# Two rounds per token gather, halved ranking matrices, nineteen weight slots and twelve rounds in an expert layer

## The chip, the cores and the metric

The kernel runs on one core of one Trainium2 chip. The metric is the time of one execution in device microseconds; the time of a kernel is the median of several executions.

## What is computed

A streaming encoder of two layers over one sequence of 256 tokens of width 1024, in fp32. The first half of each layer (band attention, a state space model, retention, one projection in and one out) is called the mixing stage here and is not changed. The second half is a hierarchical mixture of 32 experts:

```python
def _hier_moe(h, w_group, b_group, w_expert, b_expert, w_gate, w_up, w_down):
    ...
    expert_id = group_idx[:, None] * EXPERTS_PER_GROUP + top_idx        # two experts of one group per token
    combine = jnp.sum(jax.nn.one_hot(expert_id, N_EXPERTS, dtype=f32) * top_w[..., None], axis=1)
    ...
        hg = jnp.einsum('nd,edf->nef', t, w_gate[e])
        hu = jnp.einsum('nd,edf->nef', t, w_up[e])
        act = jax.nn.silu(hg) * hu * combine[:, e, None].astype(t.dtype)
        out = out + jnp.einsum('nef,efd->nd', act, w_down[e]).astype(f32)
```

An expert's weights are 3 MiB (gate and up 1024 x 256 each, down 256 x 1024), so a layer's experts are 96 MiB, and every one is read once.

## The kernel before

Weights reach the core as tiles of 128 x 2048 fp32, 1 MiB each: two for an expert's gate and up (`load_gu`, line 131, its two halves of the contraction) and one for its down projection (`load_wd`, line 138). SP issues these loads one after another, in an order that the framework sets. A tile goes into one of 17 slots in turn (`wslot`, line 121): 8 of the pool tag `ring2`, 7 of a ring that the mixing stage uses as well, 2 of the tag `ring3`. The slots of the two tags lie on memory that the mixing stage used just before; a slot is free again when the matmuls that read it are done. In layer 0 the first eight slots first hold tiles for the next layer's modulation.

A round handles 128 token slots: two experts of up to 64 tokens each, or four light ones of up to 32. `route` picks each token's two experts and each token's place in its expert's list (`posm`), all on VectorE with a few matmuls; TensorE and VectorE work there in the order written. `order` counts tokens per expert on the device and ranks the experts that are not in fixed order, with comparison matrices of 26 x 26 per partition (lines 1081 to 1092): the six largest are heavy, the other 20 light. Six experts (`FIX`) are taken in fixed order, so their weights can be loaded before the ranking is known. `ORDER` gives eleven rounds: three fixed, then light and heavy in turn three times, then two light.

Rounds are grouped in blocks whose tokens are gathered together. `matrix` builds a 0/1 selection matrix on VectorE, `gathered` multiplies it with the token rows, which are kept as two fp32r parts (`xhi`, `xlo`), eight chunks of 128 model columns, four matmuls each; ScalarE and VectorE carry the result out of PSUM with norm and modulation applied. Block 0 is the three fixed rounds (256 columns before round 0, 128 more after its gate/up), blocks 1 and 2 are four rounds each, 512 columns.

Per round, TensorE then does `slots` (two transposes that give each slot's weight `cw` and the mask `sT`), `gate_up` (fp32, experts side by side in columns of the array), `turned` (two transposes of the activations, behind ScalarE's silu and VectorE's product), `down`, and `scatter`. Before a scatter, `outputs` multiplies with the gate row on VectorE, rounds to fp32r on ScalarE and subtracts on VectorE; `scatter` multiplies both parts with the mask, and VectorE adds the result to `x`. The order on TensorE in `run` is written by hand; the other engines are ordered by the framework there. Behind a round's gate/up come the scatter and the down of earlier rounds. Between the first and the second half of the rounds stands `overflow`: all engines load the largest count and skip, or take, a branch for experts with more tokens than slots.

PSUM has four tags of two banks: gate/up and activations turn in one, down in another, and gathers, scatters and transposes share the tags `tr` and `ac`.

Of the kernel before, what the change touches and what calls it, by code (L numbers as in the profile page):

```python
# [12 lines left out]
F32R = mybir.dt.float32r  # L13
# [12 lines left out]

FIX, HEAVY, LIGHT = 6, 6, 32
DYN = NE - FIX
ORDER = ["fixed"] * 3 + ["light", "heavy"] * 3 + ["light"] * 2
EPS = 1e-6  # L30
PRIO = 200
NW = 7
NW2 = 8
NW3 = 2

# [16 lines left out]
def body(tc, I, O):  # L52
# [3 lines left out]
    with tc.tile_pool(name="cp", bufs=1) as cp, tc.tile_pool(name="ring", bufs=NW) as ring, \  # L56
# [3 lines left out]
        def nm(s):  # L60
# [6 lines left out]
                        "mx": 4, "smx": 4},  # L67
                "moe": {"ring2": NW2, "ring3": NW3, "big": 2, "b4": 1, "b2": 8, "y2": 4, "b1": 8, "cw": 3},
                "prep": {"b1": 4}}
# [887 lines left out]
        def route(l, filler, scaled):  # L957
# [5 lines left out]
            def turned(h, t):  # L963
                xT[h, t] = b2([128, 512])
                p = ps("tr")
                for c in range(4):
                    PE.transpose(p[:, c * 128:(c + 1) * 128], x[:, t, (4 * h + c) * 128:(4 * h + c + 1) * 128], ident)
                return p
# [50 lines left out]
            m1, at1, f1 = first_max(ev, "a")  # L1019
            oh1, oh2 = sb([128, 10, 8], "oh1"), sb([128, 10, 8], "oh2")  # L1020
            V.tensor_tensor(oh1, at1, wide(f1), op=ALU.is_equal)
# [24 lines left out]

            def weights():
                V.tensor_tensor(oh2, at2, wide(f2), op=ALU.is_equal)
                m5 = m1.rearrange("p (t g) -> p t g", t=2)
# [13 lines left out]
                V.tensor_tensor(w2, w1, e, op=ALU.mult)  # L1063
                wa, both = sb([128, 10, 8], "wa"), sb([128, 10, 8], "both")
                for o, oh, w in ((wa, oh1, w1), (both, oh2, w2)):
# [5 lines left out]
            def order():  # L1071
# [8 lines left out]
                V.scalar_tensor_tensor(key, cnt[:, FIX:NE], 64.0, own, op0=ALU.mult, op1=ALU.subtract)  # L1080
                sq = [128, DYN, DYN]
                tmp, oh = sb(sq, "sqa"), sb(sq, "sqb")

                rank = sb([128, DYN], "rank")
                V.tensor_tensor(tmp, key[:, None, :].to_broadcast(sq), key.unsqueeze(2).to_broadcast(sq), op=ALU.is_ge)
                V.tensor_reduce(rank, tmp, axis=AX.X, op=ALU.add)
                V.tensor_tensor(oh, C("iota")[:, 0:DYN].unsqueeze(2).to_broadcast(sq),
                                rank[:, None, :].to_broadcast(sq), op=ALU.is_equal)

                def sorted_(dst, src):  # L1090
                    V.tensor_tensor(tmp, oh, src[:, None, :].to_broadcast(sq), op=ALU.mult)
                    V.tensor_reduce(dst, tmp, axis=AX.X, op=ALU.add)

# [29 lines left out]
        def experts(posm, comb, xhi, xlo, a2, sh2, gr2, l, ahead=True, D0=None, between=None, order=None, more=True,  # L1123
# [8 lines left out]
            if ahead:  # L1132
                numi, posd, comd = order
                _, num = nc.values_load_multi_w_load_instructions(
                    numi[0:1, :], engines=(mybir.EngineType.SP,), min_val=FIX, max_val=NE - 1,
                    skip_runtime_bounds_check_because="sums of a permutation's 0/1 rows times FIX..NE-1")
                at_ = {"fixed": 0, "heavy": FIX, "light": FIX + HEAVY}
                for r, kind in enumerate(ORDER):
                    i, n, w = at_[kind], *((4, LIGHT) if kind == "light" else (2, CAP))
                    at_[kind] += n  # L1140
                    blk, po = (0, r) if i < FIX else (1 + (r - FIX // 2) // 4, (r - FIX // 2) % 4)
                    j = slice(i - FIX, i - FIX + n) if i >= FIX else slice(i, i + n)
                    pos, cmb = (posd[:, :, j], comd[:, :, j]) if i >= FIX else (posm[:, :, j], comb[:, :, j])
                    rounds.append((blk, po * 128, w, pos, cmb, [num[e - FIX] if i >= FIX else e for e in range(i, i + n)]))
            else:
                for r in range(16):
                    j = slice(2 * r, 2 * r + 2)
                    rounds.append((r // 4, r % 4 * 128, CAP, posm[:, :, j], comb[:, :, j], [2 * r, 2 * r + 1]))
            last = {r[0]: i for i, r in enumerate(rounds)}

            def gather(blk):
                Dm[blk] = b4([128, 2, 512], F32R)
                for b, po, w, pos, _, _ in rounds:
                    if b == blk:
                        matrix(Dm[blk], po, pos, w)
                gathered(blk, slice(0, rounds[last[blk]][1] + 128), 1)

            def gathered(blk, ss, n):
                pc = {}
                w = ss.stop - ss.start  # L1160
                for c0 in range(0, 8, n):
# [8 lines left out]
                    for c in range(c0, c0 + n):  # L1170
                        if (blk, c) not in hg:
                            hg[blk, c] = b2([128, 512])
                        h = hg[blk, c][:, ss]
# [5 lines left out]
            def slots(r):  # L1179
# [11 lines left out]
                V.tensor_reduce(cw, tp[:, 0:256], axis=AX.X, op=ALU.add)  # L1191
                sT = b1_([128, 256], F32R)
                V.tensor_scalar(sT, tp[:, 0:256], 0.0, None, op0=ALU.is_gt)
# [68 lines left out]
            if not ahead:  # L1262
                for r in range(16):
                    if r % 4 == 0:
                        gather(r // 4)
                    cw, sT = slots(r)
                    scatter(sT, outputs(down(r, turned(gate_up(r, cw)))))
# [11 lines left out]
            def run(rs):  # L1279
                with tc.manual_schedule(engines={mybir.EngineType.PE}):  # L1280
                    for r in rs:
                        blk, po, _, _, _, es = rounds[r]
                        if r == 0:
                            Dm[0] = D0
                            gathered(0, slice(0, 256), 4)
                        elif po == 0:
                            for q in list(aT):
                                downs(q)
                            scatters(1)
                            gather(blk)  # L1290
                        cw, sTs[r] = slots(r)
                        act = gate_up(r, cw)
                        if r == 0:
                            gathered(0, slice(256, rounds[last[0]][1] + 128), 1)
                        scatters(0)
                        for q in list(aT):
                            downs(q)
                        aT[r] = turned(act)
                        if late and r == len(rounds) - 2:
                            late()  # L1300
                        if len(es) == 4:
                            downs(r, r == len(rounds) - 1)
                            scatters(1)
                    for q in list(aT):
                        downs(q)
                    scatters(0)

            half = last[1] + 1
            run(range(half))
# [3 lines left out]
        def moe(l, more):  # L1313
# [25 lines left out]
            with tc.manual_schedule(engines={mybir.EngineType.PE, mybir.EngineType.DVE}):  # L1339
                posm, comb, cmi, r, weights, order, less = route(l, filler, scaled)  # L1340
                D0 = b4([128, 2, 512], F32R)
                matrix(D0, 0, posm[:, :, 0:4], CAP)
                for h in range(2):
                    hs = slice(h * 512, (h + 1) * 512)
                    for t in range(2):
                        V.scalar_tensor_tensor(xlo[:, t, hs], x[:, t, hs], r[:, t:t + 1], xhi[:, t, hs].bitcast(F32),
                                               op0=ALU.mult, op1=ALU.subtract)
                matrix(D0, 4 * CAP, posm[:, :, 4:FIX], CAP)
            weights()
            ordered = order()  # L1350

            def overflow():

                n = nc.values_load(cmi[0:1, 0:1], min_val=0, max_val=S)
                with tc.If(n > CAP):
                    posr = sb([128, 2, 32], "posr")
                    V.tensor_tensor(posr, posm, less.unsqueeze(1).to_broadcast([128, 2, 32]), op=ALU.add)
# [173 lines left out]
```

## Time and profile before

| what | value |
|---|---|
| median of 3 runs | 855.92 us (855.15 to 857.68) |
| profiled execution | 861.28 us |
| its span, first to last instruction | 859.4 us |
| TensorE matmul busy | 718.6 us (84%) |
| VectorE busy | 482.2 us (56%) |
| ScalarE busy | 240.3 us (28%) |
| bytes moved | 293.62 MB, mean 342 GB/s |
| mean granted clock of TensorE | 0.927 |

The busy shares are means over the whole span. The mixing stages and the expert stages have different limits, so the rows further down are taken from stretches of the span. Times in rows are microseconds from the span's start. A matmul's row is longer than the distance to the next one, since matmuls are pipelined; durations of steps are therefore read from the start of one to the start of the next. Gate/up and down matmuls are in fp32 and each shows as two records.

### The profile page before, as it was taken

The page shows a single profiled execution, that of the slowest core. Times are in us where ns is not written, and L with a number is a line of the kernel's source. Part 1 is how long each engine was busy: PE and PEld are TensorE (multiplying, and loading weights), DVE is VectorE, ACT ScalarE, POOL GpSimd, SP SyncE. Part 2 cuts the span into 40 slices and gives each one's busy share as a digit, 9 for nine tenths or more (in the row PEclk, how much of TensorE's full clock was granted, in tenths as well). Part 3 has the DMA queues.
Part 4 walks back from the last instruction along what each step waited for, and adds up shares of the span by engine and source line. Part 5 has one row for each costly group of instructions (what it writes and reads, how often), then busy time and mean ns, then how long its engine had stood idle before and what let it go on. Part 6 is the DMA issues. An engine that isn't in the chain of part 4 may idle for free. (4 is left out here: it accounts for less than half of the span.)

```text
span 859.4 us, 11389 instructions
## 1 busy us (share of the span) xinstructions
PE 718.6 (84%) x4110; PEld 390.8 (45%) x4110; DVE 482.2 (56%) x1075; ACT 240.3 (28%) x512; POOL 115.2 (13%) x163
## 2 busy tenths in 40 slices
PE   2699999989999985987678989989699998497875
PEld 0365776675434322422126558657653532242211
DVE  6689798455654334222158989855755533422124
ACT  1534236732222110101034333494321211020102
POOL 0454150002000000000035216000100000000000
PEclk9699999997999998899898989989799999899888
DMA  9978778887998998999998846759369899899992
GB/s 370 422 302 300 260 281 352 359 290 307 374 413 345 415 416 333 415 419 414 414 417 364 315 153 251 291 211 407 140 245 418 326 417 416 342 415 420 414 416 87
DMA packets 52037, 293.62 MB, mean 342 GB/s; under 512 B 4736, under 2 KB 4992, under 8 KB 26624
## 3 DMA queue, kind: packets, MB, share of 16 engines
q1 hardware_dynamic: 49536, 287.78, 84.0%
q10 hardware_dynamic: 2432, 4.98, 1.6%
q8 instruction: 36, 0.59, 0.3%
q14 instruction: 33, 0.27, 0.1%
HBM read 289.60 MB, written 1.05 MB: 338 GB/s over the span
## 5 line engine op out<-in xcount | busy, mean ns | idle before, releaser
L1204 PE MATMUL mm<-ring,b 128*32 128x512 f32 (+1 forms) x608 | 126.8, 622 | 11.8 <-DMA ring<-in_wgu_dram 11.8
L710 DVE TENSOR_TENSOR wh<-w,wh 128x512 fp32r<-128x512 f32 x120 | 85.6, 735 | 34.7 <-ACT wh L709 34.4
L1210 DVE SCALAR_TENSOR_TENSOR b<-mm,cw,b 128x256 f32<-128x256 f32 x22 | 10.6, 483 | 160.9 <-ACT b L1208 160.9
L709 ACT ACTIVATE wh<-w 128x512 fp32r<-128x512 f32 x120 | 74.4, 629 | 87.3 <-PE mm L734 49.5
L1204 PE MATMUL mm<-w,b 128*32 128x512 f32 (+1 forms) x416 | 88.8, 631 | 8.6 <-DMA w<-in_wgu_dram 8.6
L734 PE MATMUL mm<-wh,early 128*128 128x512 f32 x288 | 78.7, 417 | 1.0 <-DVE wh L710 1.0
L1229 PE MATMUL sc<-ring,b 128*32 128x512 f32 (+1 forms) x288 | 63.4, 623 | 12.8 <-DMA ring<-in_moe_w_down_dram 8.4
L1204 PEld LDWEIGHTS mm<-ring,b 128*32 128x32 f32 (+1 forms) x608 | 34.4, 124 | 77.0 <-issue 54.8
L734 PEld LDWEIGHTS mm<-wh,early 128*128 128x128 f32 x288 | 53.1, 194 | 25.2 <-issue 6.8
L205 PE MATMUL ac<-w,cc 128*32 128x512 f32 x320 | 46.2, 662 | 20.0 <-DVE cc L199 11.6
L1208 ACT ACTIVATE b<-mm 128x256 f32<-128x256 f32 x22 | 8.4, 384 | 184.3 <-PE mm L1204 184.3
L1238 DVE TENSOR_TENSOR y<-sc,gr 128x512 f32<-128x512 f32 x44 | 30.4, 690 | 50.1 <-PE sc L1229 48.6
L1243 ACT ACTIVATE y<-y 128x512 fp32r<-128x512 f32 x40 | 25.2, 630 | 107.9 <-DVE y L1238 67.1
L729 PE MATMUL mm<-early,wh 128*128 128x256 f32 x384 | 52.5, 292 | 1.7 <-DVE wh L710 1.7
L729 PEld LDWEIGHTS mm<-early,wh 128*128 128x128 f32 x384 | 48.5, 194 | 8.3 <-issue 4.1
L1168 PE MATMUL tr<-b,big 128*128 128x512 f32 (+2 forms) x128 | 32.4, 393 | 22.8 <-DVE b L1119 20.0
L734 PE MATMUL mm<-wh,big 128*128 128x512 f32 x192 | 50.2, 414 | 1.4 <-DVE y L921 1.4
L1184 POOL TENSOR_TENSOR b<-b,comd 128x128 f32<-128x128 f32 x32 | 12.8, 424 | 282.0 <-PE mm L1216 129.9
L1204 PEld LDWEIGHTS mm<-w,b 128*32 128x32 f32 (+1 forms) x416 | 23.8, 124 | 55.4 <-issue 38.9
L1229 PE MATMUL sc<-w,b 128*32 128x512 f32 (+1 forms) x224 | 44.0, 597 | 4.8 <-DMA w<-in_moe_w_down_dram 2.9
L734 PEld LDWEIGHTS mm<-wh,big 128*128 128x128 f32 x192 | 36.7, 197 | 9.6 <-DVE y L921 2.2
L1229 PEld LDWEIGHTS sc<-ring,b 128*32 128x32 f32 (+1 forms) x288 | 15.9, 123 | 48.6 <-issue 26.8
(349 smaller groups left out, 1108.9 us busy)
## 6 DMA issues: line engine op xcount, KB each, us to landing
ring<-in_wgu_dram SPq DMA_DIRECT2D x76, 1024.0 KB, 14.6
w<-in_wgu_dram SPq DMA_DIRECT2D x52, 1024.0 KB, 13.0
w<-in_w_ada_dram SPq DMA_DIRECT2D x40, 1024.0 KB, 9.0
ring<-in_moe_w_down_dram SPq DMA_DIRECT2D x36, 1024.0 KB, 18.8
w<-in_moe_w_down_dram SPq DMA_DIRECT2D x28, 1024.0 KB, 19.5
w<-in_win_dram SPq DMA_DIRECT2D x22, 1024.0 KB, 6.9
w<-in_w_out_dram SPq DMA_DIRECT2D x8, 1024.0 KB, 7.1
ring<-in_w_ada_dram SPq DMA_DIRECT2D x8, 1024.0 KB, 11.9
```

What stands on the lines that cost most here:

```text
L205: PE.matmul(acc[32 * t:32 * t + 32, :], c1[:, k:k + 1].to_broadcast([128, 32]), w[:, t * 512:(t + 1) * 512], start=(k == 0), stop=(k == 7) ...
L709: A.activation(wh[:, 0], w, AF.Copy)
L710: lo_eng[par_[0] % len(lo_eng)].tensor_tensor(wh[:, 1], w, wh[:, 0].bitcast(F32), op=ALU.subtract)
L729: PE.matmul(pt[t][:, f * 256:(f + 1) * 256], whs[i][:, w_, fs], a[x_][:, k], start=first and f + m == 0, stop=end and m == 2, skip_group_c ...
L734: PE.matmul(pt[t], a[x_][:, k, ts_], whs[i][:, w_], start=first and m == 0, stop=end and m == 2)
L1168: PE.matmul(pc[c], (xlo if i else xhi)[:, t, cs], Dm[blk][:, t, ss], start=(i + t == 0), stop=(i + t == 3))
L1184: G.tensor_tensor(Dc[:, t].rearrange("p (e s) -> p e s", s=w), Dm[blk][:, t, po:po + 128].bitcast(F32).rearrange("p (e s) -> p e s", s=w), ...
L1204: PE.matmul(gu[o:o + w, :], hg[blk, k][:, po + o:po + o + w], ws[k // 4][j][:, k % 4] if ahead else part_gu(l, es[j], k), start=(k == 0), ...
L1210: V.scalar_tensor_tensor(act, gu[:, 256:512], cw, si, op0=ALU.mult, op1=ALU.mult)
L1229: PE.matmul(yp[h][o:o + w, :], aT[:, f * 128 + o:f * 128 + o + w], wd[j][:, f, h] if ahead else part_wd(l, es[j], f, h), start=(f == 0), s ...
L1238: V.tensor_tensor(y, yp[h], gr2[:, h * 512:(h + 1) * 512], op=ALU.mult)
L1243: A.activation(yh, y, AF.Copy)
```

## The change

Slots become 19: `ring3` has four tiles for two. Eight experts are in fixed order, in four rounds; eight heavy and sixteen light ones follow in turn, so there are twelve rounds. Every block has two rounds: six gathers of 256 columns, matrices and gathered tokens in tiles of half the size (tags `D` and `hg`). The branch stands behind block 3, round 7. The ranking uses 24 x 24 comparisons done in two halves of 12 x 24, kept in the buffers of the outputs (`y2`), where the transposed tokens of the routing now lie too. Some routing tiles reuse others' memory, masks get a tag `sT` of their own, and the tag `b1` has four buffers for eight. In `run`, a block's first round now does the pending scatter before the pending down and the gather; a light round does the pending scatter before its own down. In the last layer, `late` (the final norm's gain spread over the partitions) moves in front of the last round's gate/up.

```diff
-FIX, HEAVY, LIGHT = 6, 6, 32
+FIX, HEAVY, LIGHT = 8, 8, 32
 DYN = NE - FIX
-ORDER = ["fixed"] * 3 + ["light", "heavy"] * 3 + ["light"] * 2
+
+HALF = 3
+ORDER = ["fixed"] * 4 + ["heavy", "light"] * 4
...
-NW3 = 2
+NW3 = 4
...
-                "moe": {"ring2": NW2, "ring3": NW3, "big": 2, "b4": 1, "b2": 8, "y2": 4, "b1": 8, "cw": 3},
+                "moe": {"ring2": NW2, "ring3": NW3, "big": 2, "D": 2, "hg": 8, "y2": 4, "b1": 4, "sT": 3, "cw": 3},
...
-                xT[h, t] = b2([128, 512])
+                xT[h, t] = y2([128, 512])
...
-                sq = [128, DYN, DYN]
-                tmp, oh = sb(sq, "sqa"), sb(sq, "sqb")
+
+                H = DYN // 2
+                sq = [128, H, DYN]
+
+                def square():
+                    return y2([128, 512])[:, 0:H * DYN].rearrange("p (a b) -> p a b", a=H)
+
+                halves = [slice(0, H), slice(H, DYN)]
+                tmp, ohs = square(), [square() for _ in halves]
...
+                for hv in halves:
+                    V.tensor_tensor(tmp, key[:, None, :].to_broadcast(sq), key[:, hv].unsqueeze(2).to_broadcast(sq),
+                                    op=ALU.is_ge)
+                    V.tensor_reduce(rank[:, hv], tmp, axis=AX.X, op=ALU.add)
...
                 def sorted_(dst, src):
-                    V.tensor_tensor(tmp, oh, src[:, None, :].to_broadcast(sq), op=ALU.mult)
-                    V.tensor_reduce(dst, tmp, axis=AX.X, op=ALU.add)
+                    for hv, oh in zip(halves, ohs):
+                        V.tensor_tensor(tmp, oh, src[:, None, :].to_broadcast(sq), op=ALU.mult)
+                        V.tensor_reduce(dst[:, hv], tmp, axis=AX.X, op=ALU.add)
...
-                    blk, po = (0, r) if i < FIX else (1 + (r - FIX // 2) // 4, (r - FIX // 2) % 4)
+                    blk, po = r // 2, r % 2
...
-                Dm[blk] = b4([128, 2, 512], F32R)
+                Dm[blk] = sb([128, 2, 256], "D", F32R)
...
-                            hg[blk, c] = b2([128, 512])
+                            hg[blk, c] = sb([128, 256], "hg")
...
-                sT = b1_([128, 256], F32R)
+                sT = sb([128, 256], "sT", F32R)
...
                         elif po == 0:
+                            scatters(0)
                             for q in list(aT):
                                 downs(q)
-                            scatters(1)
                             gather(blk)
+                        if late and r == len(rounds) - 1:
+                            late()
                         cw, sTs[r] = slots(r)
                         act = gate_up(r, cw)
-                        if r == 0:
-                            gathered(0, slice(256, rounds[last[0]][1] + 128), 1)
                         scatters(0)
                         for q in list(aT):
                             downs(q)
                         aT[r] = turned(act)
-                        if late and r == len(rounds) - 2:
-                            late()
                         if len(es) == 4:
+                            scatters(0)
                             downs(r, r == len(rounds) - 1)
-                            scatters(1)
...
-            half = last[1] + 1
+            half = last[HALF] + 1
...
-                D0 = b4([128, 2, 512], F32R)
+                D0 = sb([128, 2, 256], "D", F32R)
...
-                matrix(D0, 4 * CAP, posm[:, :, 4:FIX], CAP)
```

## Rows read from the trace of the kernel before

**Rows 1.** The page, the span in 40 equal slices: what the transfers moved.

```profile
GB/s 370 422 302 300 260 281 352 359 290 307 374 413 345 415 416 333 415 419 414 414 417 364 315 153 251 291 211 407 140 245 418 326 417 416 342 415 420 414 416 87
```

**Rows 2.** Stretches, layer 1: length; PE, PEld, DVE, ACT, POOL busy; clock; DMA; GB/s.

```profile
610.00:620.00 10.00, 3.33 (x19) 2.79 (x19) 9.11 (x39) 1.53 (x4) 1.19 (x2) 0.58 0.22 92
...
629.00:700.00 71.00, 68.36 (x372) 31.05 (x368) 35.79 (x66) 13.71 (x26) 3.57 (x10) 1.00 0.93 373
700.00:845.00 145.00, 112.47 (x615) 42.02 (x616) 44.81 (x81) 16.24 (x30) 3.61 (x10) 0.92 0.96 390
```

**Rows 3.** SP's waits, whole span: us in total, times, longest us.

```profile
SPq L135 <- PE mm L1204: 56.8, 14, 13.9
SPq L143 <- PE mm L1204: 50.9, 11, 22.8
...
SPq L1355 <- SPq L1355: 39.3, 10, 12.1
```

**Rows 4.** TensorE in time: first gate/up, last scatter, layers 0 and 1.

```profile
215.85 7.09 PE L1204 MATMUL mm<-w,b 128*64 128x512 f32 x32
...
437.42 1.98 PE L1256 MATMUL ac<-y,b 128*128 128x512 f32 x4
...
625.58 7.09 PE L1204 MATMUL mm<-ring,b 128*64 128x512 f32 x32
...
845.91 1.98 PE L1256 MATMUL ac<-y,b 128*128 128x512 f32 x4
```

**Rows 5.** TensorE in time, layer 1, rounds 1 and 2.

```profile
643.69 3.60 PE L1229 MATMUL sc<-w,b 128*64 128x512 f32 x16
...
647.23 0.44 PE L1216 MATMUL mm<-cst,b 128*128 128x128 f32 x2
...
647.81 7.09 PE L1204 MATMUL mm<-w,b 128*64 128x512 f32 x32
...
654.83 0.50 PE L1258 MATMUL ac<-y,b 128*128 128x512 f32 x1
...
656.90 0.64 PE L1229 MATMUL sc<-w,b 128*64 128x512 f32 x1
```

**Rows 6.** TensorE in time, two records of the scatter ahead of the branch.

```profile
737.40 0.50 PE L1258 MATMUL ac<-y,b 128*128 128x512 f32 x1
...
740.58 0.50 PE L1259 MATMUL tr<-y,b 128*128 128x512 f32 x1 [0.58 <-DVE y L1245]
```

**Rows 7.** TensorE in time, end of a gate/up and its turn.

```profile
767.10 0.60 PE L1204 MATMUL mm<-w,b 128*32 128x512 f32 x3
...
768.86 0.44 PE L1216 MATMUL mm<-cst,b 128*128 128x128 f32 x2 [1.15 <-DVE b L1210]
```

**Rows 8.** TensorE in time: gathers of 256 columns (layer 0) and 512 (layer 1).

```profile
214.07 0.63 PE L1168 MATMUL tr<-b,big 128*128 128x256 f32 x4
214.54 0.63 PE L1168 MATMUL ac<-b,big 128*128 128x256 f32 x4
...
668.35 2.40 PE L1168 MATMUL tr<-b,big 128*128 128x512 f32 x8 [1.17 <-DVE x L1260]
...
676.08 0.38 PE L1189 MATMUL tr<-cst,b 128*128 128x128 f32 x2
```

**Rows 9.** In time, behind the branch of layer 1.

```profile
748.58 2.52 DVE L1119 TENSOR_TENSOR b<-cst,posd 128x128 fp32r<-128x128 f32 x8 [6.18 <-DVEq L1355]
...
751.05 3.75 PE L1168 MATMUL tr<-b,big 128*128 128x512 f32 x8 [9.51 <-DVE b L1119]
```

**Rows 10.** In time, routing and ranking in layer 1.

```profile
606.26 0.69 DVE L986 CUSTOM_DVE_ANT_0 y<-x 128x512 f32<-128x512 f32 x1
606.50 0.98 PE L972 MATMUL sc<-prb,b 128*128 128x40 f32 x8
...
619.59 0.85 DVE L1085 TENSOR_TENSOR sqa<-key 128x676 f32<-128x676 f32 x1
```

**Rows 11.** TensorE in time, `late` in layer 1.

```profile
807.32 1.95 PE L270 MATMUL tr<-cst 128*128 128x128 f32 x16
```

More of the change, by code (lines that the diff above doesn't have):

```diff
@@ L1019, in route @@
             m1, at1, f1 = first_max(ev, "a")
-            oh1, oh2 = sb([128, 10, 8], "oh1"), sb([128, 10, 8], "oh2")
+            oh1 = sb([128, 10, 8], "oh1")
             V.tensor_tensor(oh1, at1, wide(f1), op=ALU.is_equal)
@@ L1047, in weights @@
             def weights():
+                oh2 = sb([128, 10, 8], "aa")
                 V.tensor_tensor(oh2, at2, wide(f2), op=ALU.is_equal)
@@ L1063, in weights @@
                 V.tensor_tensor(w2, w1, e, op=ALU.mult)
-                wa, both = sb([128, 10, 8], "wa"), sb([128, 10, 8], "both")
+                wa, both = sb([128, 10, 8], "ev2"), sb([128, 10, 8], "at3")
                 for o, oh, w in ((wa, oh1, w1), (both, oh2, w2)):
@@ L1080, in order @@
                 V.scalar_tensor_tensor(key, cnt[:, FIX:NE], 64.0, own, op0=ALU.mult, op1=ALU.subtract)
-                sq = [128, DYN, DYN]
-                tmp, oh = sb(sq, "sqa"), sb(sq, "sqb")
-                rank = sb([128, DYN], "rank")
[L1085 to L1088, printed above, removed]
+                H = DYN // 2
[4 more added lines that the diff above has]
+                tmp, ohs = square(), [square() for _ in halves]
+                rank = sb([128, DYN], "rank")
+                for hv in halves:
[3 more added lines that the diff above has]
+                for hv, oh in zip(halves, ohs):
+                    V.tensor_tensor(oh, C("iota")[:, hv].unsqueeze(2).to_broadcast(sq),
+                                    rank[:, None, :].to_broadcast(sq), op=ALU.is_equal)
                 def sorted_(dst, src):
-                    V.tensor_tensor(tmp, oh, src[:, None, :].to_broadcast(sq), op=ALU.mult)
-                    V.tensor_reduce(dst, tmp, axis=AX.X, op=ALU.add)
+                    for hv, oh in zip(halves, ohs):
+                        V.tensor_tensor(tmp, oh, src[:, None, :].to_broadcast(sq), op=ALU.mult)
+                        V.tensor_reduce(dst[:, hv], tmp, axis=AX.X, op=ALU.add)
                 num = sb([128, DYN], "num")
@@ L1147, in experts @@
                     j = slice(2 * r, 2 * r + 2)
-                    rounds.append((r // 4, r % 4 * 128, CAP, posm[:, :, j], comb[:, :, j], [2 * r, 2 * r + 1]))
+                    rounds.append((r // 2, r % 2 * 128, CAP, posm[:, :, j], comb[:, :, j], [2 * r, 2 * r + 1]))
             last = {r[0]: i for i, r in enumerate(rounds)}
             def gather(blk):
-                Dm[blk] = b4([128, 2, 512], F32R)
+                Dm[blk] = sb([128, 2, 256], "D", F32R)
                 for b, po, w, pos, _, _ in rounds:
@@ L1263, in experts @@
                 for r in range(16):
-                    if r % 4 == 0:
-                        gather(r // 4)
+                    if r % 2 == 0:
+                        gather(r // 2)
                     cw, sT = slots(r)
@@ L1355, in overflow @@
                 with tc.If(n > CAP):
-                    posr = sb([128, 2, 32], "posr")
+                    posr = sb([128, 10, 8], "oh1").rearrange("p n e -> p (n e)")[:, 0:64].rearrange("p (t e) -> p t e", t=2)
                     V.tensor_tensor(posr, posm, less.unsqueeze(1).to_broadcast([128, 2, 32]), op=ALU.add)
```

## Prediction

> **What bounds the kernel now.** I read the page's slices first, then stretches of the second expert layer, SP's waits, and last the instructions in order of time. The slices show transfers near 415 GB/s through most of both expert stages, the best slice 425 or less [rows 1]. One expert tile is 1 MiB, so at 419 GB/s a load takes 1.0486/0.419 = 2.5 us, and the 96 loads of a layer 240 us. The change loads no fewer bytes; what can be won is time in which the load queue stands still.
>
> It stands still in three places. Between 610 and 620 us the queue moves 92 GB/s, because all 17 slots are full and SP waits 22.8 us for the first round's matmuls [rows 2, 3]. From 629 to 700 us TensorE is busy 68.4 of 71 us and the loads run at 373 GB/s: there TensorE is the bound, slots come free at its pace, and (419-373)/419 x 71 = 7.8 us of loading is lost; SP's wait of 13.9 us belongs to the four-round gather, during which no slot comes free [rows 2, 3]. From 700 to 845 us TensorE is busy only 112 of 145 us and the loads run at 390 GB/s, which loses 10 us, mostly at the overflow branch, where SP first lets its outstanding transfers land [rows 2, 3]. So each expert stage has a TensorE-bound head and a load-bound tail with some 30 us of TensorE slack. The last scatter starts 220.3 us after the first gate/up in layer 1 (625.58 to 845.91) and 221.6 us after it in layer 0 (215.85 to 437.42) [rows 4]. These two stretches are what the change touches.
>
> **The change, part by part.**
>
> *Two more slots* let two more loads go while the queue is idle before the first gate/up: 5.0 us per layer, if the load lane decides. The added slots lie on memory of the mixing stage; the wait for it ends with that stage, before the idle stretch does, so I cost it at nothing; if it came later than that, up to 5.0 us per layer would be gone.
>
> *Gathers of 256 columns.* A four-round gather takes 668.35 to 676.08 = 7.7 us for 32 matmuls of 512 columns; at 256 columns four matmuls take 214.07 to 214.54 = 0.47 us, so 3.8 us for 32 [rows 8]. The work per layer stays the same to a microsecond; but slots are now held 3.8 us instead of 7.7, and there are five gathers behind the first one instead of three, each with its own start: 1.2 us of waiting for a PSUM bank where a scatter went ahead [rows 8].
>
> *Twelve rounds for eleven, order of scatters.* A round costs TensorE gate/up 7.0 (647.81 to 654.83), down 3.55 (643.69 to 647.23), the two small turns 0.6 (647.23 to 647.81), and a scatter 2.07 if its operands wait for it (654.83 to 656.90) [rows 5]. Where the scatter comes right behind its own down, as the new order has it in every second round and around every light one, it waits for the chain VectorE, ScalarE, VectorE: from 737.40 to about 741.4 (the second-last operand is ready at 740.58, and four of the eight products still follow at 0.2 to 0.3 us), 4.0 us [rows 6]. Such scatters stand in the trace only at the branch and at the end; I count nine of them per layer in the new order. Bounds are 2.07 (hidden) and 5.3 (half of the eight comparisons of 2.52 us that build the next selection matrix land in between [rows 9]); I take 4.25, near the row. Behind a waiting scatter TensorE holds the next down or gather, and with it the slots. Where nothing stands between gate/up and its own turn (rounds 0, 6, 8, 10) the turn ends 1.8 us after the gate/up [rows 7].
>
> *The branch* moves one round later and stays what it is: TensorE last works near 741.4, VectorE starts the comparisons at 748.58, now four instead of eight, so the gather starts near 749.8, 8.5 us idle; its first 16 matmuls run at half clock (8 of 512 columns in 3.75 us), 5.6 us for the gather [rows 6, 9].
>
> *Routing and ranking.* The square sum of line 986 takes its scratch from a buffer that the first transposed block has just used, so it waits for the first logits: 606.26 becomes about 607.5 [rows 10]; the copy behind it on VectorE and the last logits follow by some 0.7 us. Against that one comparison and the 128-column gather leave the head of the stage. Ranking in halves doubles 13 instructions of 0.85 us [rows 10] with 288 elements in place of 676 each: between 9.4 us (in proportion) and 22 us (no gain), near 12; its results are first needed by the 25th load, no longer by the 19th, and TensorE's evacuations come between. I take 0.3 us for all of it, bounds -0.5 and +3. Buffer tags that shrink (the matrix, the gathered tokens, the masks) are each reused behind an instruction that already stands ahead on the same engine; the cover is TensorE's own order, and without it each would cost a round's wait of 1 to 2 us.
>
> *The sum*, TensorE lane, from the first gate/up to the end of the last down: 12 gate/up 84.0; 12 downs 42.6; nine scatters at 4.25, 38.2; two hidden at 2.07, 4.1; gathers 4 x 3.8 + 2 x 1.2 + 5.6 = 23.2; eleven small slot transposes at 0.3, 3.4; turns 4 x 1.8 + 2 x 0.3 = 7.8; branch 8.5; routing 0.3. Together 212.1. Layer 1 has besides the 2.0 us of line 270, which moves in front of the last gate/up [rows 11]: 214.1. Against 221.6 and 220.3 that is 9.5 and 6.2 us less, 15.7 in all.
>
> The load lane as check: the 48th load reuses a slot that is free when half of round 5's gate/up is done, by the same terms 77 us after the start; then about 5.5 us for a first load on an idle queue, 48 more at 2.5 (120), and at most 6 at the branch (from the 10 us above), and 2.5 for the rest of the last down: 211. The lanes end within about 3 us of each other, so neither slack is large, and a miss in TensorE's terms shows in full. In layer 0 the end of the stage carries the mixing stage with it, since its first loads queue directly behind the last expert tile.
>
> The profiled execution is 861.28 us long, its span 859.4; less 15.7 it would be 845.6. The median of the runs is 855.92, 5.4 below, so I expect 840.
>
> **A rule against it.** In the stretch from 629 to 700 us, with several waits of about 1 us in it, the granted clock is 1.00, the upper level of 2.4 GHz; it is 0.92 on average from 700 to 845, where TensorE waits long [rows 2]. The Trainium skill, "TensorE: Matmul & The Clock Gate", section "HAM oscillation — how this bites in real kernels", says that idle gaps let the array fall to half rate, so that the next burst starts cold, and that a kernel with such gaps in its loop pays at every turn. By that rule the nine new waits would each be followed by slow matmuls; by the rows waits of 1 to 2 us leave the clock up. By the one the time would be 873 (worked out under C), by the other 840; I go by the rows.
>
> **Rivals.**
>
> A, the other side: *the scatter's chain gets longer.* The place is lines 1238 to 1260 behind every down; VectorE does there two products, two subtractions, four additions and, new in that spot, evacuations and comparisons. The gain of 7.9 us per layer is eaten when each of the nine waits costs 0.9 us more, 5.1; at 5.3, the upper bound, the run comes out at 840 + 18 x 1.05 = 859; from 5.3 on it is slower. Against it: the same chain took 4.0 with two additions in between.
>
> B: *the loads come later*, by the memory under the new slots or by the branch. The load lane's 211 us become 216 to 218 per layer, 2 to 6 us behind TensorE's, and 840 becomes 846 to 850. For it: SP issues in order, and one late slot holds all behind it.
>
> C: *the clock falls in each new wait.* A first stretch at half clock costs 3.75 instead of about 1.9 us [rows 8, 9]; nine times per layer 17 us: 840 + 33 = 873.
>
> D: *waits hide.* Scatters at 3.0 and ranking at nothing: the TensorE lane loses 11 us, the load lane, which then binds, 3 to 5: about 831.
>
> E: the change does nothing, because load time alone counts: then the 10 us at the branch and the drain stay, the two slots are used up by the longer head: 853 to 858. Against it: the TensorE-bound head.
>
> **How the numbers follow.** Chances: forecast (833 to 848) 0.58, B 0.16, D 0.06, E 0.09, A 0.08, C 0.03. The range takes the forecast, B and D: 831 to 853. A measurement of this kernel tells 0.3%, 2.6 us, from no change. Faster: forecast, B, D and a part of E, 0.82; the same: the rest of E and a part of A, 0.08; slower: 0.10.
>
> **What would show it.** The distance from first gate/up to last scatter falls to about 212 and 214 us. Four-round gathers are gone and SP's longest wait for gate/up inside a stage falls from 13.9 to below 8 us. The load rate from the first scatters on, 373 and 390 GB/s in the two stretches, rises to 390 or more in both. Scatters behind their own down take about 4.2 us. If they take 5 or more, A; if TensorE waits for weights from round 4 on, B; if the granted clock inside rounds falls well under 0.9, C. The forecast is wrong above all if the nine waits are mis-sized, since each 0.1 us there is 1.8 us of the whole.

## The result and the profile after

The changed kernel takes 846.43 us (median), the one before 856.8 in the runs beside it: a ratio of 0.9896, 95% interval 0.9853 to 0.9938. It is faster by 1%, about 10 us where 16 were forecast; 846 lies in the predicted range, on rival B's times (846 to 850) and 6 above the forecast's 840. Its profiled execution took 853.19 us, with a span of 851.4 us.

TensorE in time, first gate/up (L1218) and last scatter (L1270) of both layers, as in [rows 4] (where the stretch asked for ends inside a group, the row counts only a part of it; the starts are what is read here):

```profile
220.04 1.51 PE L1218 MATMUL mm<-w,hg 128*64 128x512 f32 x6
...
437.65 0.70 PE L1270 MATMUL ac<-y,sT 128*128 128x512 f32 x1
...
622.64 0.65 PE L1218 MATMUL mm<-ring,hg 128*64 128x512 f32 x2
...
838.35 1.99 PE L1270 MATMUL ac<-y,sT 128*128 128x512 f32 x4
```

The stages last 217.6 and 215.7 us, 4.0 and 4.6 less than before; 212.1 and 214.1 were forecast. The mixing stage between them is 3.2 us shorter too (188.2 to 185.0). The change does not touch it, and in the runs below it takes 182.2 to 185.7 us whichever part of the change they leave out, 183.4 in the old kernel with only its scatters moved: the 188.2 stand in the one profiled execution of before alone, and why is not shown. Against that the first gate/up comes 4.2 us later than before (220.04 for 215.85), 1.7 of them in the routing; the last section has the granted clock there.

Stretches of layer 1, columns as in [rows 2]:

```profile
622.00:630.00 8.00, 7.45 (x35) 2.41 (x34) 7.62 (x22) 2.11 (x4) 1.00 (x2) 1.00 0.34 111
630.00:710.00 80.00, 74.35 (x394) 32.55 (x394) 37.25 (x74) 14.81 (x30) 3.79 (x10) 1.00 0.99 389
710.00:740.00 30.00, 26.76 (x178) 11.69 (x178) 11.71 (x21) 4.29 (x8) 0.76 (x2) 1.00 1.02 416
740.00:750.00 10.00, 8.88 (x54) 3.30 (x54) 5.86 (x10) 2.03 (x4) 0.00 (x0) 1.00 0.52 193
750.00:833.00 83.00, 68.45 (x406) 30.88 (x398) 31.62 (x60) 13.83 (x26) 3.19 (x8) 0.94 1.01 414
```

The head now loads at 389 GB/s. That is not yet the measure of the forecast, whose stretches of before began 3.4 us behind the first gate/up and took in the branch and the end. The same stretches of the changed kernel:

```profile
626.00:697.00 71.00, 65.65 (x324) 29.46 (x320) 36.42 (x74) 12.98 (x26) 3.04 (x8) 1.00 0.97 380
697.00:838.00 141.00, 120.09 (x740) 50.85 (x740) 54.61 (x99) 22.17 (x42) 4.71 (x12) 0.96 0.94 383
```

So 373 became 380 and 390 became 383, where 390 or more was forecast for both. The landings of the loads in the trace agree, counted from the first gate/up of layer 1: the 48th landed at 91.1 us before and at 86.6 now, the last at 216.7 and at 212.1. The second half of the loads takes 125.7 and 125.6 us. All that layer 1 gained, it gained in the first half.

The largest loss that is left is the hole at the overflow branch: 193 GB/s for 10 us is (419-193)/419 x 10 = 5.4 us without loading. Before, the hole was 4.0 us (2.7 + 1.3):

```profile
735.00:740.00 5.00, 4.35 (x17) 1.44 (x13) 3.34 (x6) 1.26 (x2) 0.00 (x0) 1.00 0.48 195
740.00:745.00 5.00, 0.96 (x3) 0.49 (x3) 1.80 (x3) 0.00 (x0) 0.00 (x0) 0.98 0.86 310
```

SP's waits of the changed kernel's stage (from 628 us) show the same place:

```profile
SPq L137 <- PE mm L1218: 33.5, 10, 6.7
...
SPq L1366 <- SPq L1366: 18.0, 3, 13.1
```

The wait of 13.9 us for a gate/up [rows 3] is gone, the longest is 6.7; the longest wait at the branch (L1366) is 13.1.

The end of both stages of the changed kernel, TensorE in time:

```profile
429.14 1.12 PE L1243 MATMUL sc<-ring,b 128*32 128x512 f32 x6
432.40 0.72 PE L1243 MATMUL sc<-w,b 128*32 128x512 f32 x1 [2.15 <-DMA w<-in_moe_w_down_dram]
...
832.24 1.15 PE L1243 MATMUL sc<-ring,b 128*32 128x512 f32 x6
834.80 3.62 PE L1243 MATMUL sc<-ring,b 128*32 128x512 f32 x26 [1.41 <-DMA ring<-in_moe_w_down_dram]
```

The last down waits for its weights: the loads end the stage, not TensorE. A down takes 3.57 us where nothing is late and a gate/up 7.0; the last two downs take 4.4 and 8.5 us in layer 0, and in layer 1 the last gate/up and the last two downs take 7.9, 5.1 and 6.1. That is 5.8 and 5.0 us more than without late weights; of the 5.8, 1.7 go to a lower clock behind the wait (below).

### The profile page after: what moved, and what is told of

Same layout as the page of the kernel before. It is cut to its first block, busy times and chain, and to the rows that moved or that the text cites. A ratio compares the mean times of both kernels' runs of the same rounds, so it can differ in the third digit from the quotient of the medians.

```text
span 851.4 us, 11748 instructions
## 1 busy us (share of the span) xinstructions
PE 729.7 (86%) x4262; PEld 404.8 (48%) x4262; DVE 503.1 (59%) x1143; ACT 250.6 (29%) x536; POOL 117.8 (14%) x167
## 5 line engine op out<-in xcount | busy, mean ns | idle before, releaser
L1218 PE MATMUL mm<-ring,hg 128*64 128x512 f32 (+1 forms) x608 | 120.9, 594 | 0.0
L1218 PE MATMUL mm<-w,hg 128*32 128x512 f32 (+1 forms) x416 | 86.1, 595 | 0.0
L1243 PE MATMUL sc<-ring,b 128*32 128x512 f32 (+1 forms) x360 | 73.1, 612 | 1.9 <-DMA ring<-in_moe_w_down_dram 1.9
L1218 PEld LDWEIGHTS mm<-ring,hg 128*64 128x64 f32 (+1 forms) x608 | 35.5, 124 | 59.2 <-issue 58.1
L207 PE MATMUL ac<-w,cc 128*32 128x512 f32 x320 | 48.0, 691 | 16.4 <-DVE cc L201 11.5
L1252 DVE TENSOR_TENSOR y<-sc,gr 128x512 f32<-128x512 f32 x48 | 33.2, 692 | 37.1 <-PE sc L1243 34.9
L1257 ACT ACTIVATE y<-y 128x512 fp32r<-128x512 f32 x44 | 27.7, 629 | 90.6 <-DVE y L1252 90.6
L1198 POOL TENSOR_TENSOR b<-D,comd 128x128 f32<-128x128 f32 x32 | 12.5, 411 | 290.8 <-PE tr L1203 114.6
L1182 PE MATMUL tr<-D,big 128*128 128x256 f32 x192 | 35.3, 329 | 17.9 <-DVE D L1133 15.9
L1218 PEld LDWEIGHTS mm<-w,hg 128*32 128x32 f32 (+1 forms) x416 | 24.9, 123 | 43.1 <-issue 41.3
L1182 PEld LDWEIGHTS tr<-D,big 128*128 128x128 f32 x192 | 30.2, 225 | 25.6 <-issue 19.3
L1243 PEld LDWEIGHTS sc<-ring,b 128*32 128x32 f32 (+1 forms) x360 | 19.9, 125 | 45.8 <-issue 38.2
```

The lines of the kernel that those rows point to most:

```text
L207: PE.matmul(acc[32 * t:32 * t + 32, :], c1[:, k:k + 1].to_broadcast([128, 32]), w[:, t * 512:(t + 1) * 512], start=(k == 0), stop=(k == 7) ...
L1182: PE.matmul(pc[c], (xlo if i else xhi)[:, t, cs], Dm[blk][:, t, ss], start=(i + t == 0), stop=(i + t == 3))
L1198: G.tensor_tensor(Dc[:, t].rearrange("p (e s) -> p e s", s=w), Dm[blk][:, t, po:po + 128].bitcast(F32).rearrange("p (e s) -> p e s", s=w), ...
L1218: PE.matmul(gu[o:o + w, :], hg[blk, k][:, po + o:po + o + w], ws[k // 4][j][:, k % 4] if ahead else part_gu(l, es[j], k), start=(k == 0), ...
L1243: PE.matmul(yp[h][o:o + w, :], aT[:, f * 128 + o:f * 128 + o + w], wd[j][:, f, h] if ahead else part_wd(l, es[j], f, h), start=(f == 0), s ...
L1252: V.tensor_tensor(y, yp[h], gr2[:, h * 512:(h + 1) * 512], op=ALU.mult)
```

## The experiments

Two theories are tested: **L**, the load lane (the 96 loads of a layer, one behind the other) ends the stage, so only what it loses counts; **T**, TensorE's lane does. Ratios are to the kernel before in the runs beside each experiment (its medians there are 854.9 to 855.9 us), in brackets the 95% interval.

**The changed kernel again.** 

> The changed kernel as it is, as the measure for the three others on the same chip. Every theory expects 0.99 of the kernel before, 846 to 848 us, a first gate/up to last scatter distance near 216 us in both layers, and TensorE waiting 4 to 6 us for weights in the last two rounds of each layer.

846.51 us, 0.9898 [0.9867, 0.9928]: the measure for the others. Its stages are 220.1 and 214.9 us.

**17 slots.** `-NW3 = 4` `+NW3 = 2`. 

> Undoes one part: 17 weight slots again. Theory L (the load lane ends each expert stage, because it loses some 5 us per layer at the branch and 6 us in the head): two loads of 2.5 us move behind the first gate/up in each layer, so each stage is 5 us longer and the run 856 us, the whole gain gone. Rival T (TensorE's lane ends it, the 5 us of waits for weights in the last rounds are chance): 847 to 849 us.

855.07 us, 1.001 [0.9986, 1.0035]: L (856), not T (847 to 849). The loss is 8.6 us; two loads of 2.5 us in each layer are 10 if the loads end the stage. Layer 1 loses it at the start: its 48th load lands 90.6 us behind the first gate/up, nearly as before (91.1), the last at 215.6.

**No branch.** `-between()`, both halves in one `run`. 

> Leaves out the overflow branch and the experts' rounds under it (the part of the computation for more than 64 tokens per expert). In the changed kernel the load queue loses 4.7 us at it in layer 0 and 5.4 us in layer 1, and TensorE is idle 7.1 us and runs the gather behind it 2 us slower. Theory L: 10 us less in all, 836 us. Rival T: 18 us less, 828 us.

835.95 us, 0.9788 [0.9759, 0.9817]. L again (836), not T (828). This kernel leaves out the rounds for experts with more than 64 tokens, so it is a measure and no alternative.

**The scatter's place.** 

> Puts the scatters back behind the next down, as in the kernel before; everything else stays changed. In the changed kernel nine scatters per layer take 4.0 us, in the new place they take some 2.1. Theory L: TensorE's lane gets some 15 us per layer shorter, but the loads end the stage, and only the bubbles of the load queue between 630 and 710 us shrink (5.7 us per layer are lost there), so 2 to 4 us per layer: 838 to 843 us, with 15 us of waits for weights now spread over the rounds behind the branch. Rival T: 15 us per layer, 817 us.

```
 elif po == 0:
-    scatters(0)
     for q in list(aT): downs(q)
+    scatters(1)
     gather(blk)
 ...
-scatters(0)
 downs(r, r == len(rounds) - 1)
+scatters(1)
```

854.5 us, 1.0002 [0.9977, 1.0026]: 8 us slower than the changed kernel, where both theories expected a gain. TensorE in time, round 3's turn (L1230) to the end of the next gather (L1203), first in the changed kernel run again, then here:

```profile
672.20 0.44 PE L1230 MATMUL mm<-cst,b 128*128 128x128 f32 x2
672.40 0.48 PE L1272 MATMUL ac<-y,sT 128*128 128x512 f32 x1
...
676.24 3.65 PE L1243 MATMUL sc<-ring,b 128*64 128x512 f32 x16
...
679.82 1.21 PE L1182 MATMUL tr<-D,big 128*128 128x256 f32 x8
...
683.74 0.38 PE L1203 MATMUL tr<-cst,b 128*128 128x128 f32 x2
```

```profile
676.81 0.44 PE L1230 MATMUL mm<-cst,b 128*128 128x128 f32 x2
...
677.78 3.65 PE L1243 MATMUL sc<-ring,b 128*64 128x512 f32 x16 [0.53 <-ACT b L1232]
...
681.36 0.50 PE L1272 MATMUL ac<-y,sT 128*128 128x512 f32 x1
...
684.67 0.74 PE L1182 MATMUL tr<-D,big 128*128 128x256 f32 x4 [1.19 <-DVE x L1274]
...
689.32 0.38 PE L1203 MATMUL tr<-cst,b 128*128 128x128 f32 x2
```

11.5 us against 12.5. The scatter itself is shorter behind the down (2.1 for 3.8), but three losses appear: 0.5 us for ScalarE's copy of the turned activations, which the early scatter had covered, 1.2 for VectorE's additions ahead of the gather, and a gather of 4.65 us for 3.9. At this place the stalled scatter of the new order costs less than what it covers. More is lost at the end of the stage:

```profile
836.84 6.53 PE L1243 MATMUL sc<-ring,b 128*32 128x512 f32 x26 [1.41 <-DMA ring<-in_moe_w_down_dram]
...
843.30 0.50 PE L1272 MATMUL ac<-y,sT 128*128 128x512 f32 x1
...
845.41 2.32 PE L1270 MATMUL ac<-y,sT 128*128 128x512 f32 x4
```

Here the scatter of the last round but one comes behind the last weights (2.1 us); in the new order it is done while TensorE waits for them anyway. Besides, the last weights come later, counted from the first gate/up: 217.3 us for 214.9 in layer 0, 213.7 for 211.4 in layer 1. The other pair of runs that differs in the order alone, with 17 slots in both (**17 slots** above, **Both undone** below), shows the same: 219.4 for 217.1 and 218.3 for 215.7, and again 2.1 us behind them. That is 4.4 to 4.7 us per layer, some 9 in all, and the ratios of the two pairs differ by 0.0104 and 0.0106, 9 us.

The 26 matmuls ahead of the scatter take 6.5 us here, against 3.6 in the changed kernel, at a granted clock of 0.54:

```profile
831.00:836.80 5.80, 2.66 (x6) 0.41 (x6) 1.25 (x2) 0.83 (x2) 0.00 (x0) 0.92 0.75 299
836.80:843.30 6.50, 6.46 (x27) 1.35 (x27) 0.00 (x0) 0.00 (x0) 0.00 (x0) 0.54 0.00 0
```

This is not shown to belong to the order: the other run with the old place has 3.6 us there, and the changed kernel itself has 5.25 in layer 0. The execution took 860.76 us, 6 above its kernel's median.

**Both undone.** 

> Undoes two parts at once: 17 slots, and the scatters behind the next down as before; gathers for two rounds and twelve rounds stay. Each of the two alone brought the time back to that of the kernel before (855 and 854.5 us). If both delay the load lane, which ends the stage, their losses add: 863 us. If one covers the other (the stage ends with the longer of two lanes): 855 us.

866.1 us, 1.0116 [1.0071, 1.0161]: the two losses add up (0.9898 + 0.0112 + 0.0104 = 1.0114). So the rest of the change (twelve rounds, gathers for two, the ranking in halves, the smaller buffers) makes the old kernel 1.2% slower by itself; slots and scatters pay for that and for the gain. Which part of the rest costs it stays open: the two that are undone below, with the new scatter place kept, cost nothing there.

**Four-round gathers, 17 slots.** The first block's second half is gathered behind the first gate/up, `blk, po = r // 4, r % 4`. 

> Undoes two parts: 17 slots and gathers for four rounds (the second half of the first block behind the first gate/up, as before); twelve rounds and the new place of the scatters stay. To be compared with the run with 17 slots alone, 855 us. Theory L: a gather of 7.7 us during which no slot comes free stops the load queue about 4 us longer than one of 3.9 us, at the two gathers in the head that are not the first, so 4 to 8 us per layer: 863 to 871 us. Rival: the same columns are gathered in all and the slots of the rounds between come free sooner, so 855 us.

854.64 us, 0.998 [0.995, 1.001], no loss against 17 slots alone (1.001): the rival holds, and L's 863 to 871 is missed. The long gather without free slots, on which a part of the forecast rested, costs nothing in the sum; with 19 slots this was not run.

**The old kernel with the new scatter place.** 

> The kernel before with one part of the change alone: each scatter ahead of the next down. With everything else changed this part was worth 8 us. If it is worth that by itself (it shortens TensorE's pair of rounds by about 1 us and frees the down slots earlier): 848 us. If it pays only with gathers for two rounds, 856 us; if the scatters that now wait for VectorE cost what the forecast put on them, 2 us each, more than 860 us.

853.38 us, 0.996 [0.9922, 0.9997]: between the cases, some 3 us (the interval allows 0.3 to 7). The order is a gain there too, but the 8 us need the rest; how the other 5 are divided stays open.

**Eleven rounds.** `FIX, HEAVY = 6, 6` and the old order. 

> Undoes one part: six experts in fixed order and eleven rounds in the old order (three fixed, light, heavy, light, heavy, light, heavy, light, light); gathers for two rounds, 19 slots and the new place of the scatters stay. One round less is some 15 us less for TensorE per layer (gate/up 7.0, down 3.6, scatter 3.8 to 4.5, small turns 0.6), against the same 96 loads. Theory L (the loads end the stage): only bubbles of the head can go, 2 to 4 us per layer: 839 to 843 us. Rival T (TensorE's lane sets the end): 817 us. Rival S (a light round needs 12 of 19 slots at once, so early light rounds make TensorE wait and slots come free in lumps): 850 us or more.

848.08 us, 0.9879 [0.9834, 0.9924]: no difference from twelve, so L's gain (839 to 843) is missed as well as T's. From 630 to 710 us the loads run without a bubble:

```profile
630.00:710.00 80.00, 73.17 (x434) 31.09 (x436) 36.15 (x71) 13.34 (x27) 3.79 (x10) 1.00 1.02 417
```

But with six fixed experts the loads from the 17th on need the ranking: they go at 627 us instead of 602 (SP, layer 1), three loads or 7.5 us of loading late, against some 5 us won in the head.

**Eleven rounds with eight fixed.** `FIX, HEAVY = 8, 4`, five light rounds. 

> The changed kernel with four heavy experts for eight and five light rounds for four: eleven rounds, of which four are fixed, so that the loads for all 19 slots still go without the ranking (with six fixed experts three of the first 19 loads waited for it). The matmul work is 15 us per layer less than with twelve rounds, the 96 loads are the same. Theory L: the load lane ends the stage; it gains only what it loses in the head to a late TensorE, 4 to 5 us per layer: 837 to 841 us. Rival T: 817 us. Rival S (light rounds in a row behind the branch free slots in lumps of 12): 846 us or more.

844.59 us, 0.9859 [0.9805, 0.9914]: its interval overlaps that of the changed kernel, and L's 837 to 841 is missed. The expectation went against its own reason: the round taken away lies behind the branch, so the head stays the same (393 GB/s from 630 to 710 us, 391 in the changed kernel run again), and the 15 us of TensorE turn into longer gate/ups and downs behind the branch, nearly all in the last two rounds, where TensorE waits for weights. T is out: 15 us of matmul work per layer are worth some 3 us in the whole run, no more than the measurement's uncertainty.

**Four tiles on GpSimd's queue.** At the branch SP waits for eight semaphores of its own transfers, the last at 743.7 us in the changed kernel run again, and issues its next load at 744.0; GpSimd is past its branch at 723.

```
-ws = [[load_gu(l, e, h) for e in es] for h in range(2)]
+ws = [[load_gu(l, e, h) for e in es] for h in range(2)] if r != half + 1 else []
+if r == half + 1:
     ...                 # ep: the same experts' numbers, read by GpSimd
+    ws = [[load_gu(l, e, 0, G) for e in ep], [load_gu(l, e, 1) for e in es]]
```

> The changed kernel, but GpSimd's own queue loads four of the tiles of the second round behind the overflow branch, since SP issues nothing from the branch until its last transfer has landed, and GpSimd is past its branch 20 us earlier. Nothing is left out. Theory L: the hole of 5 us in the transfers at the branch fills in both layers, and the run takes 837 to 839 us; the transfer rate stays above 390 GB/s through the branch. Rival T (TensorE's own 7 us of idleness at the branch are what costs): 846 us with a filled hole. Rival Q (two queues share the engines, so SP's drain only ends later by what the other queue takes): the hole moves and stays, 846 us.

852.52 us, 0.9956 [0.9916, 0.9995]: slower than the changed kernel, but its two layers differ, and that tells. Layer 0, 340 to 355 us, the changed kernel and this one:

```profile
340.00:345.00 5.00, 4.20 (x19) 1.56 (x15) 3.60 (x6) 1.64 (x3) 0.00 (x0) 1.00 0.28 82
345.00:350.00 5.00, 4.68 (x36) 1.61 (x36) 2.59 (x5) 0.63 (x1) 0.00 (x0) 1.00 0.93 360
350.00:355.00 5.00, 2.71 (x8) 1.16 (x7) 4.11 (x7) 0.63 (x1) 0.00 (x0) 0.93 1.02 433
```

```profile
340.00:345.00 5.00, 4.52 (x21) 1.70 (x17) 3.33 (x6) 1.65 (x3) 0.00 (x0) 1.00 1.01 418
345.00:350.00 5.00, 4.37 (x36) 1.47 (x36) 2.92 (x5) 0.32 (x1) 0.00 (x0) 1.00 1.02 424
350.00:355.00 5.00, 3.40 (x16) 1.34 (x8) 3.96 (x7) 0.94 (x2) 0.00 (x0) 1.00 0.94 357
```

The hole of 4.7 us is down to 0.7, the stage to 213.7 us, and its last down waits for nothing. In layer 1 the four loads stood behind GpSimd's branch and its next products (759.74 for 330.42 us, GpSimd in time):

```profile
330.42 0.77 POOL L137 DMA_DIRECT2D ring<-in_wgu_dram  x1 [26.54 <-PE mm L1224]
...
759.74 0.64 POOL L137 DMA_DIRECT2D ring<-in_wgu_dram  x1 [0.28 <-issue]
```

There a gate/up waits 8.5 us for them, and the stage takes 219.4. So the next run issues the same loads ahead of the branch in GpSimd's order, 25 to 36 us earlier:

```
 run(range(half))
+kept = [wslot() for _ in range(4)]          # the round behind the branch
 ...
+over = [load_gu(l, e, 0, G) for e in ep]    # the round after it
 between()
```

> The run with four tiles on GpSimd's queue again, with these four issued ahead of GpSimd's own branch in both layers (in the run before, they stood ahead of it in layer 0 alone, whose stage fell to 213.7 us with no wait for weights at its end, and behind it in layer 1, where they came 30 us too late). Nothing is left out. Theory L: 4 to 6 us less in layer 0 and 2 to 5 us in layer 1, 837 to 840 us, and the transfer rate through the branch above 350 GB/s in both layers. Rivals T and Q as before: 846 us.

838.73 us, 0.9802 [0.9749, 0.9855]: faster than both kernels, with nothing left out, as L has it (837 to 840). The stages take 215.4 and 213.5 us, together 4.4 us less than in the changed kernel's profile and 6.2 less than in that of its run again; the medians differ by 7.8, and where the remainder lies is not shown. Layer 1 at the branch, and its last down:

```profile
730.00:740.00 10.00, 8.77 (x54) 3.06 (x50) 6.53 (x10) 2.27 (x4) 0.00 (x0) 1.00 0.98 406
740.00:750.00 10.00, 2.44 (x7) 1.15 (x7) 3.77 (x6) 0.63 (x1) 0.00 (x0) 0.71 0.88 333
```

```profile
819.23 3.64 PE L1246 MATMUL sc<-ring,b 128*32 128x512 f32 x32
822.80 1.55 PE L1273 MATMUL ac<-y,sT 128*128 128x512 f32 x3
```

The hole is 2.4 us instead of 5.4, and the last down of layer 1 runs without a wait: there TensorE's lane ends the stage, at 213.5 us; in layer 0 one wait of 1.8 us is left in the last down. The Trainium skill, "DMA: Bandwidth & Descriptors", section "Issuing engines are not separate DMA queues", says that issuing on several engines only saves the sequencer's time to start a transfer, usually little. The trace agrees that two queues move no more than one (418 to 424 GB/s in the rows above); but SP's sequencer stands still for long at this branch, 19 us from one load to the next (728.74 to 748.00 in the changed kernel).

**Both together.** 

> The two before together: four of the loads over the branch on GpSimd's queue, and eleven rounds with eight fixed experts. Nothing is left out. Theory L: the two gains are of the same lane at different places and add up, 828 to 833 us. Rival (one covers the other): 838 us.

845.12 us, 0.9855 [0.9808, 0.9903]: they do not add up, and neither L (828 to 833) nor the rival (838) has it. The gate/up of the second round behind the branch and the last two downs wait for weights, and the hole is 3.3 us (280 GB/s from 740 to 750 us). With three light rounds in a row behind the branch, 36 tiles are due there; why the filled hole gains nothing in that order is open.

Over all of them, L's times came true for 17 slots, no branch and GpSimd's loads ahead of the branch, and were missed for the scatter's place, the four-round gathers, both runs with eleven rounds and both changes together. That late loads end the stage is shown; what a saving of TensorE's gives the loads, L did not foretell.

## Why the prediction was right in sign and too large

**The step that failed** is the check by the load lane, 211 us, "the lanes end within about 3 us of each other". It ran 217.6 and 215.7. Term by term in layer 1, from the first gate/up at 622.64: the 48th load went at 701.10, 78.5 us instead of 77. It took 8.1 us to land and not 5.5, since the queue was not idle (the three loads ahead of it landed until 704.6). The 48 behind it, branch included, took 125.6 us, where 120 + 6 were taken. The last down took 3.55 behind the last weights (834.80) instead of 2.5, since the four experts alternate in it and 26 of its 32 matmuls stand behind the last tile. That is 1.5 + 2.6 - 0.4 + 1.0 = 4.7 us. In layer 0 the last weights were there 212.4 us after the first gate/up, 3.9 later than in the sum, and the last down took 5.25 us behind them, at a granted clock of 0.67, a mean of both levels:

```profile
425.00:432.40 7.40, 4.13 (x17) 1.73 (x17) 4.37 (x7) 1.01 (x2) 0.00 (x0) 1.00 1.03 416
432.40:437.60 5.20, 5.20 (x26) 1.25 (x26) 0.69 (x1) 0.00 (x0) 0.00 (x0) 0.67 1.01 418
```

**TensorE's sum held** within 3.4 us. Without what the late weights cost, the stages would be 217.6 - 5.8 = 211.8 and 215.7 - 5.0 = 210.7, forecast 212.1 and 214.1; in the run with GpSimd's loads ahead of the branch, where no weight of layer 1 was late, its stage took 213.5. The nine scatters took 3.8 to 4.5 (4.25 taken); the branch cost 7.1 us of idleness and a gather of 6.1 (8.5 and 5.6 taken). Rival A, which hung on these waits being longer, fell, and D, which hung on their being shorter.

**What the sum could not show.** The forecast took the longer lane by its own figures, TensorE's, and that lane came out the shorter. B's outcome, late loads at 216 to 218 us per layer, is the one that happened, but by neither of B's causes: the first loads into the new slots went at 604.5 to 605.8 us, well ahead, and the branch cost 5.4 us in layer 1 and 4.7 in layer 0, within the 6 that the lane already held. The loads came later at the 48th, at its landing and at the end. With two lanes 1 to 3 us apart on paper, and misses of 3.4 and 4.7 us in them, 0.16 for B against 0.58 was too little. The result lies at the upper edge of the forecast's own band (833 to 848), but not because TensorE's lane ends the stage, as the forecast had it, nor for B's reasons: to that extent the hit is luck.

**The rates of before** were read a little wrongly too. Of the 10 us of loading lost from 700 to 845 us, "mostly" at the branch, the rows above show 4.0 there, and the last weights were there at 842.4, so 2.6 us more are only the end of the stage.

**The reasons for the gain** were partly wrong. The two slots were right, 5 us per layer forecast, and undoing them costs 8.6 us in all. The shorter gathers were wrong: four-round gathers cost nothing. The scatters were counted as a loss of TensorE and are a gain of 8 us in the changed kernel: the rows of before showed what a scatter costs in either place [rows 5, 6], not which waits of its neighbours it covers.

**The routing** was right in size. From the first transposes to the first gate/up it is 28.3 us in layer 0 before and in the changed kernel run again, at the same granted clock of 0.82 (30.0 at 0.77 in the profile shown above). In layer 1 it is 21.1 before at 0.68 and 19.8 now at 0.74; the run with 17 slots and four-round gathers, with the changed routing, has 21.1 at 0.68 again, so these 1.3 us go with the clock.

**C and the rule.** The granted clock is 1.00 from 622 to 750 us, with a scatter in every second round that waits twice for 0.5 to 0.6 us, so C fell. It was lower where TensorE stood still for longer, at the branch and behind it, and in layer 0's last down behind a wait of 2.15 us (above), though not in layer 1's behind one of 1.41:

```profile
755.50:762.00 6.50, 0.01 (x1) 0.00 (x0) 1.26 (x4) 0.00 (x0) 0.00 (x0) 0.62 1.01 420
762.00:770.00 8.00, 7.54 (x40) 6.70 (x42) 4.65 (x13) 2.26 (x4) 1.68 (x4) 0.67 1.01 418
```

The loop in the section of the Trainium skill that the prediction names, "TensorE: Matmul & The Clock Gate", "HAM oscillation — how this bites in real kernels", waits for its data at every turn for longer than it computes. The short waits here are no case of it, so the prediction's reading of it went further than the page.

## What to carry to other kernels

Where two lanes end within a few us, forecast both with the same care, put a doubt on each, and give the other lane its chance; then ask of each edit which lane it shortens. In a stage that loads end, matmul work behind the last weights costs its full time (2.1 us for a scatter here), while 15 us of it taken away ahead of them were worth some 3, so put ahead of them what can stand there. Compare rates over stretches that lie alike in the stage and hold the same parts of it. Here a branch that lets a queue drain cost a hole of about 5 us in the transfers, and four loads from an engine that issued them ahead of its own branch brought it to 2.4.

## What the runs showed of the hardware

The granted clock in layer 0's routing differs between executions of nearly the same code: from 190 to 198 us it was 0.54 in the changed kernel run again and 1.00 in the run without the branch, with TensorE busy throughout in both (rows below, in this order), and routing took 28.3 and 23.5 us. Over the fourteen profiled executions of this case it took 23.2 to 23.5 us in four, at a mean clock of 1.00, 28.3 in six, at 0.82, and 30.0 to 30.3 in four, at 0.72 to 0.77: the kernel before and the changed kernel run again are in the second group, the changed kernel's first profile in the third. Why is not shown. Single profiles are therefore compared stage by stage, not by their spans.

```profile
190.00:198.00 8.00, 8.00 (x42) 6.26 (x41) 1.08 (x4) 2.46 (x4) 2.28 (x2) 0.54 1.03 403
```

```profile
190.00:198.00 8.00, 8.00 (x75) 4.67 (x78) 4.32 (x22) 2.48 (x6) 1.87 (x2) 1.00 1.02 414
```

At the branch of layer 1 TensorE's queue stands 5.8 us in one compare-and-branch, and VectorE is idle 5.5 us there, though no instruction of the branch's body is in the trace; SP's longest wait there is 11.3 us in this run and 13.1 in the profile shown above, at semaphores of its own transfers. Two records of the changed kernel run again:

```profile
L1366 SPq EVENT_SEMAPHORE  x8: 17/17/17, 738.5 to 743.7; - x8
...
L1366 PEldq COMPARE_BRANCH  x1: 5832/5832/5832, 753.0 to 753.0; - x1
```
